# Short-sequence attention: larger load packets for q, k and v, paid for with more selector matmuls, and a reordered end

## The chip, the cores and the metric

One core of a Trainium2 chip runs the whole kernel. The metric is the device time of one execution in microseconds, lower is better. Executions of this kernel scatter by two to three per cent (148.55 to 153.12 us in one set of runs), and a run is called slow when it is more than 1.5% above the fastest run of the same kernel; comparisons use fast runs.

## The reference, cut to what matters

```python
# q, k, v: float32 [32, 12, 128, 64]: 384 heads of 128 positions by 64
scores = (1 / sqrt(64)) * q @ k.transpose(0, 1, 3, 2)
attn   = softmax(scores)            # over the last axis
out    = attn @ v                   # float32
```

Each head needs q, k and v read once (37.75 MB in all) and its result written once (12.58 MB). Nothing is reused between heads, so the kernel is a stream.

## The kernel before

A unit is eight heads, and there are 48 units. The loads convert float32 to bf16 on the way and are issued by POOL. A partition takes R = 8 consecutive rows of q or k (2 KB read in one piece) or RV = 4 rows of v (1 KB). Having several rows in one partition makes longer pieces, but it puts the rows in an order that the matmuls can't use directly. For q and k the transposes put that right. For v, PE multiplies with columns of the identity ("pick"), which gathers one row from each of the 32 partitions of a head into one 32-row tile; four such matmuls bring all its rows. These are the parts that matter here:

```python
R, RV = 8, 4                     # rows per partition: q and k, v
PERIOD, LOOP0, TRIPS = 8, 2, 5   # PE's program: steps 2..41 are a loop of 8 steps,
                                 # the others are written out
NQ, NVB, NO = 12, 2, 3           # buffers for q (and k), for v groups, for outputs

def order_v(m):                  # PE: bring v of one unit into row order
    ...
    for i in range(nh):          # nh = 4 // n, n units in the load group
        h = w * nh + i
        for r in range(RV):      # 4 matmuls of 512 columns for n = 4
            x = nc.tensor.matmul(
                t[r * SV:(r + 1) * SV, i, :, :],
                lhsT=pick[:, h * SV:(h + 1) * SV],
                rhs=v_b[g % NVB][:, :n * 2, r * D:(r + 1) * D],
                start=True, stop=True)

def tensor_step(u):              # cut: PE's order in one step
    transposes(u + 3)            # 8 matmuls, q or k of a coming unit
    order_v(u + 4)               # 4 matmuls
    scores(u + 1)                # 8
    values(u)                    # 32

# POOL, for a v load: its buffer must have been read by PE
if x >= NVB:
    last = sum(vgroups[:x - NVB + 1]) - 1
    g_.wait_ge(pe_act, ev_pe_act["V", last])
```

In a step, ACT copies the ordered v out of PSUM (`keep_v`) and takes the exponentials, and DVE copies the transposed q and k, pairs up the next ones and normalises. SP stores two units at a time. A v load needs a buffer that PE has finished ordering, and there are two such buffers of four units each. That is the link from PE back to the transfers.

The softmax here doesn't subtract the row's maximum and nothing guards it: scores larger than these inputs give would overflow.

## Time and profile before

| | before |
|---|---|
| time, median of three runs | 150.04 us (149.95 to 150.37) |
| span of the profiled execution | 147.9 us |
| PE instructions by the page (matmuls / weight loads) | 2528 / 2528 |
| DMA engines' time lost until 135 us, by fitted packet costs | 5.9 us, all of it before 50 us |

"Time lost" is worked out from the packet records: for each stretch of 5 us, 5 us less (packets in it x fitted cost) / 16 engines. The prediction explains the fit. A loss of zero means that the sixteen engines always had a packet to move. What bounds the kernel is in the page's slices and in the waits, which the prediction shows.

### The profile page before, as it was taken

How to read it: one execution, taken by the hardware profiler on the slowest of the kernel's cores; microseconds unless marked ns; L12 is line 12 of the kernel's file. 1: busy time of each engine (PE TensorE's matmuls, PEld its weight loads, DVE VectorE, ACT ScalarE, POOL GpSimd, SP SyncE). 2: the span in 40 equal slices, each digit the busy share in tenths (PEclk: the TensorE clock that was granted, in tenths of full speed). 3: DMA queues.
4: the chain of work that ended last, by engine and by line, in shares of the span. 5: the costliest groups of instructions: out<-in, count | busy, mean ns of one | idle time of the engine just before them, and what ended most of it. 6: DMA issues, size and time to landing. Idle time of an engine off the chain costs nothing. (4 is left out here: it accounts for less than half of the span.)

```text
span 147.9 us, 5753 instructions
## 1 busy us (share of the span) xinstructions
PE 99.3 (67%) x2528; PEld 65.8 (44%) x2528; DVE 91.1 (62%) x202; ACT 74.9 (51%) x97; POOL 47.3 (32%) x67
## 2 busy tenths in 40 slices
PE   0247779975298859719949929829819949984530
PEld 0234436553255536415736616516515725653420
DVE  1242347877188966727868937837927858897240
ACT  3005645658047857714746736725824746766510
POOL 6912727054009091270063090090093010010000
PEclk9999999999659996985796895996985796899555
DMA  1999999999999999999999999999999999997442
GB/s 14 197 180 200 149 185 221 223 210 254 244 211 235 203 248 246 248 233 223 239 226 241 243 227 233 246 225 232 243 228 233 237 224 244 236 283 230 145 136 71
DMA packets 38282, 31.59 MB, mean 214 GB/s; under 512 B 1408, under 2 KB 38272, under 8 KB 38272
## 3 DMA queue, kind: packets, MB, share of 16 engines
q0 software_dynamic: 25568, 18.88, 83.3%
q1 hardware_dynamic: 12704, 12.58, 29.3%
q8 instruction: 6, 0.10, 0.2%
q14 instruction: 4, 0.03, 0.1%
HBM read 37.75 MB, written 12.58 MB: 340 GB/s over the span
## 5 line engine op out<-in xcount | busy, mean ns | idle before, releaser
L214 PE MATMUL qk_ps<-ident,pair 128*128 128x128 bf16 x384 | 38.3, 260 | 32.6 <-PEq L204 32.6
L311 ACT CAST v_e<-v_ps 128x512 bf16<-128x512 f32 x48 | 28.2, 588 | 62.3 <-PE v_ps L229 62.3
L318 ACT ACTIVATE attnT<-s_ps 128x1024 bf16<-128x1024 f32 x48 | 49.3, 1027 | 3.6 <-PE s_ps L250 3.6
L214 PEld LDWEIGHTS qk_ps<-ident,pair 128*128 128x128 bf16 x384 | 29.1, 117 | 37.4 <-issue 36.0
L192 POOL DMA_DIRECT2D v_b<-in_v_dram x14 | 12.3, 882 | 81.4 <-PE v_ps L229 48.0
L352 DVE COPY qkT<-qk_ps 128x1024 bf16<-128x1024 bf16 x48 | 33.0, 688 | 8.1 <-PE qk_ps L214 8.0
L369 DVE TENSOR_TENSOR o_sb<-o_ps,recip 128x512 f32<-128x512 f32 x48 | 33.2, 691 | 1.7
L260 PE MATMUL o_ps<-v_e,attnT 128*32 128x65 bf16 x1536 | 25.0, 214 | 8.6 <-issue 5.2
L229 PE MATMUL v_ps<-v_b,pick 128*32 128x512 bf16 (+2 forms) x224 | 23.9, 448 | 2.4 <-PEq L204 2.4
L260 PEld LDWEIGHTS o_ps<-v_e,attnT 128*32 128x32 bf16 x1536 | 18.1, 108 | 15.8 <-issue 12.8
L250 PE MATMUL s_ps<-qkT 64*128 64x128 bf16 x384 | 22.9, 251 | 0.0
L366 DVE RECIPROCAL recip<-o_ps 128x8 f32<-128x8 f32 x48 | 9.8, 204 | 20.8 <-PE o_ps L260 19.9
L345 DVE COPY pair<-k_b 128x1024 bf16<-128x1024 bf16 x24 | 10.8, 451 | 17.4 <-DMA v_b<-in_v_dram 17.3
L250 PEld LDWEIGHTS s_ps<-qkT 64*128 64x128 bf16 x384 | 13.0, 106 | 13.7 <-issue 13.2
L178 POOL DMA_DIRECT2D k_b<-in_k_dram x24 | 18.0, 750 | 0.0
L174 POOL DMA_DIRECT2D q_b<-in_q_dram x24 | 17.6, 733 | 1.0 <-SPq L82 1.0
L345 DVE COPY pair<-q_b 128x1024 bf16<-128x1024 bf16 x24 | 10.1, 419 | 1.7 <-DMA q_b<-in_q_dram 1.7
L229 PEld LDWEIGHTS v_ps<-v_b,pick 128*32 128x32 bf16 x224 | 5.8, 102 | 10.1 <-issue 7.3
L311 ACT ACT_TABLE_LOAD x1 | 1.3, 1283 | 0.9 <-SPq L82 0.9
L383 DVE COPY pick<-ident 128x128 bf16<-128x128 bf16 x1 | 0.2, 227 | 2.0 <-POOL ident L167 2.0
L378 DVE MEMSET ident<- 128x64 uint32 x1 | 0.1, 112 | 1.0 <-SPq L82 1.0
L167 POOL TENSOR_SCALAR_AFFINE_SELECT ident<-ident 128x128 bf16<-128x128 bf16 x1 | 0.3, 312 | 0.1
(5 smaller groups left out, 0.7 us busy)
## 6 DMA issues: line engine op xcount, KB each, us to landing
out_dram<-o_sb SPq DMA_DIRECT2D x22, 512.0 KB, 7.8
q_b<-in_q_dram POOLq DMA_DIRECT2D x24, 256.0 KB, 14.0
k_b<-in_k_dram POOLq DMA_DIRECT2D x24, 256.0 KB, 15.2
v_b<-in_v_dram POOLq DMA_DIRECT2D x11, 512.0 KB, 12.2
out_dram<-o_sb SPq DMA_DIRECT2D x4, 256.0 KB, 4.6
v_b<-in_v_dram POOLq DMA_DIRECT2D x1, 256.0 KB, 5.8
v_b<-in_v_dram POOLq DMA_DIRECT2D x2, 128.0 KB, 9.7
```

The lines of the kernel that those rows point to most:

```text
L174: g_.dma_start(out=q_b[x % NQ][:], in_=qs[:, 2 * x:2 * x + 2, :]).then_inc(s_q[x % NQ], 16)
L178: g_.dma_start(out=k_b[x % NQ][:], in_=ks[:, 2 * x:2 * x + 2, :]).then_inc(s_k[x % NQ], 16)
L192: g_.dma_start(out=t, in_=src).then_inc(s_v[x % NVB], 16)
L214: i = nc.tensor.transpose(qk_ps[:, :, r4, jj, :], x[:, r].rearrange("p a d -> p (a d)"), ident[:])
L229: x = nc.tensor.matmul(t[r * SV:(r + 1) * SV, i, :, :], lhsT=pick[:, h * SV:(h + 1) * SV], rhs=v_b[g % NVB][:, :n * 2, r * D:(r + 1) * D], ...
L250: i = nc.tensor.matmul(s_ps[u % 2][:, a, h, :], lhsT=x[p, 1, 4 * w + h, :], rhs=x[p, 0, 4 * w + h, :], start=True, stop=True)
L260: i = nc.tensor.matmul(o_ps[h * SV:(h + 1) * SV, a, r * (D + 1):(r + 1) * (D + 1)], lhsT=x[:, a, h, r * SV:(r + 1) * SV], rhs=v_of(u, a, h ...
L311: nc.scalar.copy(v_e[m % NVE][:, :, :D], v_ps[:].rearrange("p (n e) -> p n e", e=D),).then_inc(act_pe, 1)
L318: nc.scalar.activation(out=attnT[u % NA][:].rearrange("p a h (r s j) -> p (a h r) s j", s=SP, j=J), in_=s_ps[u % 2][:].rearrange("p a h (r ...
L345: nc.vector.tensor_copy(pair[t % NP][:], src[s % NQ][:].rearrange("p a (r d) -> p r a d", d=D),).then_inc(dve_pe, 1)
L352: nc.vector.tensor_copy(qkT[s % NT][:, j].rearrange("p h x -> p (h x)"), qk_ps[:].rearrange("p h r j s -> p (h r j s)"),).then_inc(*((dve_ ...
L369: nc.vector.tensor_mul(o[:, :, w, :].rearrange("p a (r d) -> p a r d", d=D), o4[:, :, :, :D], r[:].unsqueeze(3).to_broadcast([128, 2, RV, D]),
```

## The change

Its intent is fewer and larger load packets. q and k go by 16 rows per partition for the forty units in the middle (4 KB pieces in place of 2 KB) and stay at 8 rows for the first and last four units; v goes by 8 rows (2 KB in place of 1 KB). With 8 rows in a partition only 16 partitions hold a head of v, and a 32-row tile has to be put together from two halves. So each ordering takes two accumulated matmuls per tile, each over half as many columns: 16 matmuls where there were 4. The last four units are reordered so that v comes last there. PE's loop starts at step 7 in place of step 2. Most stores of two units go out as two transfers in place of one, and the two-unit v groups have buffers of their own.

The core of the diff (most of the rest moves the same waits into an explicit list of operations; cuts are marked "..."):

```diff
-    R = 8
-    RV = 4
+    RO, SO = 4, S // 4
+    RV, SV = 8, S // 8
+    for R in [8] * 2 + [16] * ((NU - 8) // 4) + [8] * 2:
...
-    vgroups = [2] + [4] * ((NU - 4) // 4) + [1, 1]
+    vgroups = [2, 2] + [4] * ((NU - 8) // 4) + [2, 2]
-    PERIOD, LOOP0, TRIPS = 8, 2, 5
+    PERIOD, LOOP0, TRIPS = 8, 7, 4
-    NQ, NVB, NVE, NP, NT, NA, NO = 12, 2, 8, 4, 4, 4, 3
+    NQ, NVB, NVE, NP, NT, NA, NO = 6, 2, 8, 4, 4, 4, 3
...
+        nh = 8 // n
         for i in range(nh):
-            for r in range(RV):
-                x = nc.tensor.matmul(
-                    t[r * SV:(r + 1) * SV, i, :, :],
-                    lhsT=pick[:, h * SV:(h + 1) * SV],
-                    rhs=v_b[g % NVB][:, :n * 2, r * D:(r + 1) * D],
-                    start=True, stop=True)
+            for jv in range(2):
+                for r4 in range(4):
+                    x = nc.tensor.matmul(
+                        t[r4 * 32:(r4 + 1) * 32, i, :, :],
+                        lhsT=pick[:, w * nh + i, jv, :],
+                        rhs=v_b[v_slot(g)][:, :n, (4 * jv + r4) * D:(4 * jv + r4 + 1) * D],
+                        start=jv == 0, stop=jv == 1)
...
+    u = TAIL                     # the last four units, written out in a new order
+    ...
```

## The prediction

> **What bounds the kernel now.** I read the page's slices first, then its queue table, then the trace's packet records by size, then windows, waits and the timeline of the end. One unit is eight heads; there are 48.
>
> ```profile
> PE   0247779975298859719949929829819949984530
> DVE  1242347877188966727868937837927858897240
> PEclk9999999999659996985796895996985796899555
> DMA  1999999999999999999999999999999999997442
> ...
> q0 software_dynamic: 25568, 18.88, 83.3%
> q1 hardware_dynamic: 12704, 12.58, 29.3%
> ```
>
> The DMA row is full from the second slice to the thirty-sixth, while PE, DVE and ACT dip to 2 and 1 again and again. The two queues' packet times add to more than 100%, so packets of the loads (q0) and of the stores (q1) overlap, and a packet's own duration is not what it costs. To get the cost I counted packets by size (v: 512 B written from 1 KB read; q and k: 1 KB from 2 KB; stores: 1 KB) in 28 windows of 2.5 us between 60 and 130 us, and fitted 16 engines x 2.5 us = sum of count x cost. The fit gives 42.1 ns for a v packet, 79.9 for a q or k packet, 53.1 for a store packet, and misses a window by 0.008 us rms: the engines were never short of work there. Over the whole run this is 12,288 x (42.1 + 79.9 + 53.1) / 16 = 134.4 us of a 147.9 us span. Summed from the start, the time the engines lost is 5.9 us by 50 us (3.5 in the first five, before loads flow; 1.4 between 15 and 25), then nothing until 135 us.
>
> ```profile
> 60.00:130.00 70.00, 50.66 (x1329) 33.83 (x1314) 48.04 (x103) 38.63 (x52) 21.61 (x29) 0.80 1.24 235
> ```
>
> Columns: PE, PEld, DVE, ACT, POOL busy, then clock, DMA share and GB/s. In these 70 us no compute engine passes 73%; 52 matmuls a unit make 1329/52 = 25.6 units, 2.74 us each by this count (some records can be missing); the packet costs give 256 x 175.1 / 16 = 2.80 us a unit.
>
> ```profile
> POOL v_b L192 <- PE v_ps L229: 48.0, 8, 9.4
> ...
> PE qk_ps L214 <- PEq L204: 32.6, 30, 5.9
> ...
> DVE pair L345 <- DMA v_b<-in_v_dram: 17.3, 8, 3.4
> ```
> ```profile
> 120.91 0.43 DVE L345 COPY pair<-k_b 128x1024 bf16<-128x1024 bf16 x1 [1.69 <-DMA v_b<-in_v_dram]
> ...
> 124.24 0.62 PE L229 MATMUL v_ps<-v_b,pick 128*32 128x512 bf16 x4
> ...
> 124.79 0.61 PE L250 MATMUL s_ps<-qkT 64*128 64x128 bf16 x8
> ...
> 126.78 0.40 PE L229 MATMUL v_ps<-v_b,pick 128*32 128x512 bf16 x4
> ...
> 127.11 0.40 PE L250 MATMUL s_ps<-qkT 64*128 64x128 bf16 x8
> ...
> 133.58 0.61 PE L214 MATMUL qk_ps<-ident,pair 128*128 128x128 bf16 x8 [0.52 <-PEq L204]
> ...
> 143.20 0.69 DVE L369 TENSOR_TENSOR o_sb<-o_ps,recip 128x512 f32<-128x512 f32 x1
> ```
>
> The waits (us in total, times, longest) show the rhythm: POOL issues a v load only when PE has freed its buffer, DVE stalls some 2 us for v once per four units, and PE behind it. The timeline of the end (start us, us) shows the last of these. At 120.91 the copy that also waits for the last group of four v units starts: the last wait for a load. From there on compute sets the pace: 23.0 us to the last normalisation's end at 143.9, and 4.0 us more for its store and the program's end. So the end is (arrival of the last four-unit v group) + (compute that remains). PE shows two speeds: v ordering to scores takes 0.55 us at 124.24 and 0.33 us at 126.78. A full step is 2.6 us slow and 1.82 to 1.9 us fast, where DVE's 0.20 + 0.69 + 0.69 + 0.42 us per unit is the limit.
>
> **What the Trainium skill says.** "DMA: Bandwidth & Descriptors", section "Why small descriptors are slow (HBM only)": a fixed overhead of about 3 cycles per packet inside the engine. "Advanced Engine Details and Errata", section "DMA Bandwidth Details": 27.2 GB/s per engine, so 37.6 ns per KB read. The fit agrees: 42.1 and 79.9 split into 4.2 ns a packet and 37.8 ns per KB. "DMA: Bandwidth & Descriptors", section "Queues, rings and completion order": an engine goes round its queues packet by packet; no run here has shown yet what that does to larger packets. "TensorE: Matmul & The Clock Gate", section "Part 1: The HAM clock gate (the "warmup" mystery)": the array runs at half clock after an idle window of some 3.4 us; the granted clock of 0.80 and the two speeds above agree.
>
> **The change part by part.**
>
> 1. Load packets. Of 48 units, 40 take q and k by 16 rows (4 KB read) and 8 stay at 8 rows; v goes by 8 rows (2 KB). A 4 KB packet costs, by the split, 4.2 + 4 x 37.8 = 155.5 ns. Loads before: 12,288 x (42.1 + 79.9) / 16 = 93.7 us. After: v 6,144 x 79.9 = 491 us, q and k 5,120 x 155.5 = 796 us and 2,048 x 79.9 = 164 us, together 1,451 / 16 = 90.7 us. Gain 3.0 us. Bytes are unchanged, so halving the packets buys only the 4.2 ns each: this is the part where a hope from "half the packets" fails. Stores keep 1 KB packets: 12,288 x 53.1 / 16 = 40.8 us, unchanged.
>
> 2. Start. Before, the third v load waits for PE (issued at 13.7 us) and the engines lose 1.4 us around it. The new order has 16 units of q and k and 12 of v before the first load that waits. I take 1.9 us less lost.
>
> 3. Arrival of the last four-unit v group. Before (units 42 to 45), 46 units of v and 42 of q and k precede or are it: (11,776 x 42.1 + 10,752 x 79.9) / 16 = 84.7 us; with 34.3 units of stores counted by then (29.2) and 5.9 lost this is 119.8, and about 1.1 us of landing gives the 120.9 seen. After (units 40 to 43): 44 units of each, 83.0 us; one unit of stores fewer, 28.3; lost 4.0. Sum 115.3, with landing 116.4: 4.5 us earlier.
>
> 4. PE's v ordering. Four matmuls of 512 columns on four 32-column tiles become 16 of 256 (two accumulated per key block): twice the columns, so the 0.33 us fast becomes about 0.33 + 512/2.4 GHz = 0.55 us, and 0.55 slow becomes about 0.98. In the middle this is 44 x 0.2 to 0.4 us of PE time that lies under the DMA: a fast step becomes 1.95 us, a slow one 3.04, and four of them mixed about 9.9 us against 4 x 2.74 = 11.0 us of DMA (estimates from the rows above).
>
> 5. Compute after that arrival. One more step remains than before (37 to 43, then the tail). Steps 37 and 38: 1.95 each if fast, about 1 us more for each slow one. Steps 39 and 40 have no transposes: PE 0.55 + 0.33 + 0.45, ACT 0.59 + 1.02; 1.7 each. Steps 41 to 43 have no v ordering: 1.82 each. Sum 12.8 to 13.9, plus 0.6 to the first transposes. Tail from the last transposes: nine DVE steps (five normalisations of 0.93, the qkT copy 0.69, three v copies of about 0.66 moved there from ACT) and PE between them; walking the chain copy, values, normalise gives 10.2 us fast and about 11.4 slow, against 10.3 (133.58 to 143.9) before, which held two v orderings and not four. Total 23.6 to 25.9 against 23.0.
>
> Sum: 143.9 - 4.5 + (0.6 to 2.9) = 140.0 to 142.3; plus 4.0 for the store and end gives a span of 144.0 to 146.3; plus the 2.2 us between span (147.9) and time (150.04): 146.2 to 148.5. I take 147.1.
>
> **The rivals.**
>
> A: the descriptors were the bound, and half of them are gone. If a packet cost its recorded duration (60 and 98 ns median) the split would be 22 ns a packet, 36 a KB, and the loads would fall by about 16 us: 136 to 140. Against it stands the fit: the durations overlap and over-count, and 37.8 ns per KB leaves little to gain.
>
> B: PE takes over. If slow steps of 3.04 us become the rule, PE passes DMA's 2.74 us a unit and the middle grows by up to 0.3 x 40 = 12 us: 152 to 158. For it: the clock is 0.80 already. Against it: shorter waits mean fewer slow stretches, and in slices 9, 10 and others PE ran above 90%.
>
> C: the gain is real but eaten at the end: slower v ordering and four of them in the tail cost as much as the 4.5 us. 149 to 151. For it: everything after 120.9 us is compute, which the change does not shorten.
>
> D: 4 KB load packets push the 1 KB stores aside in the turn of queues; o_sb's three buffers fill and DVE waits. Stores took 7.8 us to land, and three buffers of two units leave some 11 us: a wait of a microsecond here and there, hidden while loads bound. Smaller than 1 us.
>
> **Range and chances.** Mechanism 1 is firm to 0.5 us, 2 and 3 to 1.5 us, 5 to 1.5 us. Together about 2.4 us either way, which covers C and part of B; A I give one in fifteen. Range 144.0 to 150.2. The 2% line lies at 147.04, just under my value, so chances: faster 0.49, same 0.46, slower 0.05.
>
> **What would show it.** Step 1: load packets near 157 ns of cost per 4 KB in a fit of windows, the loads' total near 91 us, DMA row still full. Step 2: no dip in GB/s near 15 to 25 us. Step 3: the last wait for v at about 116 us. Step 4: 16 matmuls per v ordering, and PE's busy time up by 10 to 20 us, waits for v smaller but still there. Step 5: from the last transposes to the end of the last normalisation 10 to 11.5 us. I would be wrong if the DMA row opened in the middle (B), if 4 KB packets cost much more or less than 155 ns, or if the DVE copy into 16-element runs took longer than 0.69 us.

## The result, and the profile after

| | before | after |
|---|---|---|
| time, median | 150.16 us (149.95 to 150.37) | 161.97 us (158.49 to 162.44) |
| ratio of fast runs | | 1.0615, 95% interval 1.0508 to 1.0722 |
| profiled span | 147.9 us | 156.3 us |
| DMA engines' time lost by 85 us | 5.9 us | 12.9 us |

A ratio here is the mean time of one kernel's fast runs over that of the other kernel's fast runs of the same rounds, so it isn't quite the ratio of the medians. After has two fast runs, 158.49 and 160.3 us; its other three took 161.7 to 162.4 at a granted clock that was no lower (0.89 to 0.91 against 0.88). Before ran at 0.81 to 0.86 in the sets below, so a lower clock is not what made after slow. The profile is of the fastest. The kernel became slower by some 6%, where 2% faster was predicted.

The page of the kernel after, the rows that answer to those of before (slices of 3.9 us, then the queues):

```profile
PE   0257776548198784879879497577598687587750
DVE  3345444448156693647988458557755985684570
PEclk9999999999758999677999969999969999955576
DMA  1999999999994999997999999999999999953043
GB/s 19 182 196 209 206 213 226 224 247 132 211 227 145 142 217 272 233 220 213 147 203 239 246 237 250 244 236 238 244 237 242 244 240 245 291 182 134 4 152 121
...
q0 software_dynamic: 13984, 18.88, 70.1%
q1 hardware_dynamic: 13024, 12.59, 27.0%
q8 instruction: 13, 0.21, 0.5%
```

The load queue's packets fell from 25568 to 13984, as intended. But the DMA row, full before until the thirty-sixth slice, opens in the middle, and the GB/s row falls to 132 and 142 to 147 where no slice from the sixth to the thirty-seventh went under 185. From about 80 us on it is full again. The last row is the queue that fetches instructions; before it had 6 packets by the page, now 13.

Two windows of each kernel give the size. The columns are the window, its length, busy time (and count) of PE, PEld, DVE, ACT and POOL, the granted clock, the DMA share and GB/s. Before:

```profile
80.00:130.00 50.00, 37.28 (x981) 24.80 (x978) 34.96 (x75) 28.40 (x38) 14.05 (x19) 0.81 1.23 235
25.00:80.00 55.00, 40.49 (x1064) 26.93 (x1052) 38.38 (x83) 31.16 (x41) 19.10 (x25) 0.83 1.23 232
```

After:

```profile
80.00:130.00 50.00, 37.79 (x1224) 26.60 (x1216) 34.08 (x75) 28.52 (x38) 11.60 (x16) 0.93 1.14 241
...
25.00:80.00 55.00, 39.44 (x1160) 27.38 (x1164) 33.00 (x73) 28.04 (x37) 8.72 (x12) 0.88 1.02 204
```

Between 80 and 130 us, with the engines saturated in both, the larger packets give 241 GB/s against 235, 2.6% more. That is the gain the prediction worked out (134.4 to 131.4 us, 2.2%). Between 25 and 80 us the rate is 204 against 232. At 52 and 64 matmuls a unit the PE counts make 1064/52 = 20.5 units before and 1160/64 = 18.1 after. PE issued 9% more matmuls in these 55 us and still got 2.3 units less done.

Why did the engines run dry? These are waits of the kernel after (engine, line, what it waited for: us in total, times, longest):

```profile
POOL v_b L425 <- PE v_ps L186: 86.6, 8, 21.0
...
DVE recip L267 <- DMA out_dram<-o_sb: 12.3, 8, 2.3
...
PE o_ps L223 <- issue: 11.5, 6, 3.3
...
DVE pair L249 <- DMA v_b<-in_v_dram: 0.4, 1, 0.4
```

DVE's wait for v, 17.3 us before, is all but gone: in the middle compute no longer waits for loads. It is the reverse. POOL waits up to 21 us for PE to free a v buffer, and it issues in order, so the q and k loads behind that v load wait too. In total POOL waited little longer than before (86.6 against 81.4 us); the difference is that before still had enough loads under way during its waits (9.4 us at most), and after had not. Two POOL stretches in the timeline of after (start, length, what it is, idle before it):

```profile
33.04 0.76 POOL L425 DMA_DIRECT2D v_b<-in_v_dram  x1 [21.00 <-PE v_ps L186]
33.79 0.72 POOL L440 DMA_DIRECT2D q_b<-in_q_dram  x1
34.48 0.74 POOL L440 DMA_DIRECT2D k_b<-in_k_dram  x1
48.66 0.76 POOL L425 DMA_DIRECT2D v_b<-in_v_dram  x1 [13.43 <-PE v_ps L186]
```

After the k load issued at 34.5 us no load was issued until 48.7 us, and the losses fall into the stretches 35 to 40, 45 to 50, 50 to 55, and again 70 to 75 and 75 to 80 us.

So PE was late. The timeline of PE in after, the groups of one step being transposes (L172), v ordering (L186), scores (L211) and values (L223):

```profile
32.10 0.62 PE L186 MATMUL v_ps<-v_b,sel 128*32 128x256 bf16 x16
32.66 0.40 PE L211 MATMUL s_ps<-qkT 64*128 64x128 bf16 x8
32.98 0.33 PE L223 MATMUL o_ps<-v_e,attnT 128*32 128x65 bf16 x19
35.52 0.29 PE L223 MATMUL o_ps<-v_e,attnT 128*32 128x65 bf16 x13 [2.21 <-issue]
...
36.30 0.62 PE L186 MATMUL v_ps<-v_b,sel 128*32 128x256 bf16 x16
...
39.30 0.31 PE L223 MATMUL o_ps<-v_e,attnT 128*32 128x65 bf16 x15
42.90 0.46 PE L223 MATMUL o_ps<-v_e,attnT 128*32 128x65 bf16 x17 [3.30 <-issue]
```
```profile
44.25 1.04 PE L186 MATMUL v_ps<-v_b,sel 128*32 128x256 bf16 x16
```

A values group is 32 matmuls that need the same inputs. Here it breaks off after 19 and after 15 of them, with no semaphore in between, and goes on 2.2 and 3.3 us later; "issue" says that the profile shows nothing that PE waited for. Each of these two stops has a 16 KB packet on the instruction queue in it: packets start at 33.24 and 40.68 us, where PE's last matmuls end at 33.32 and 39.60, take 0.95 us, and PE resumes 1.3 us after they end. From one stop to the next, PE's records (matmuls, weight loads and its sequencer's waits) number 256 each time, for all seven stops between 29 and 67 us: one stop per 16 KB block, at 64 bytes each. After the longer stop PE runs at about half speed for nearly two steps (v ordering takes 1.04 us at 44.25), after the shorter it doesn't (0.62 us at 36.30). The record of the granted clock goes to half at 41.36 us and back at 48.19, in stretches that are multiples of 3.41 us: the length agrees with the window of the clock gate that the prediction names, but the half clock came 1.8 us after PE had stopped, not after 3.4 us of idling.

The Trainium skill, "Runtime: NRT & Kernel Launch", section "Instruction fetch mechanics", says that instructions come in 16 KiB blocks of 256, fetched by a DMA queue of the sequencer's own, and that the cost is mostly hidden. The trace agrees on the block's size, and disagrees on the hiding: between 20 and 80 us there are seven such stops in after, 12.8 us together (idle time of PE that the timeline puts down to "issue", stops over 0.4 us).

Before had them too, but fewer:

```profile
39.62 0.35 PE L260 MATMUL o_ps<-v_e,attnT 128*32 128x65 bf16 x11 [3.73 <-issue]
```

That and one of 0.62 us are all between 20 and 80 us, because its loop begins at step 2 and, once inside it, PE runs code that is there already (no instruction packet between 45 and 133 us). After has 64 matmuls a step in place of 52 and enters the loop five steps later, so it fetches more.

The times at which units are normalised, from the trace, show where the loss builds up:

| unit | before, us | after, us | difference |
|---|---|---|---|
| 0 | 18.0 | 20.1 | +2.1 |
| 4 | 29.6 | 35.9 | +6.3 |
| 16 | 60.5 | 73.2 | +12.7 |
| 37 | 121.3 | 127.3 | +6.0 |
| 47 | 143.0 | 151.5 | +8.5 |

By unit 16 after is 12.7 us late. Before is paced by its transfers there and later, so after catches up in part until unit 37; what remains corresponds to the engine time that was lost for good. 7.0 us more lost, less the 2.3 us that larger packets save by then (3.0 x 37/48), is 4.7 of those 6.0 us. I have not placed the other 1.3. The last ten units add 2.5 us; the third set shows that they are a second place where the loss arises.

### The profile page after: what moved, and what is told of

Its sections match the earlier page's. It is cut to its first block, busy times and chain, and to the rows that moved or that the text cites. A ratio compares the mean times of both kernels' runs of the same rounds, so it can differ in the third digit from the quotient of the medians.

```text
span 156.3 us, 7154 instructions
## 1 busy us (share of the span) xinstructions
PE 106.6 (68%) x3200; PEld 76.4 (49%) x3200; DVE 93.2 (60%) x210; ACT 73.0 (47%) x94; POOL 31.0 (20%) x47
## 3 DMA queue, kind: packets, MB, share of 16 engines
q0 software_dynamic: 13984, 18.88, 70.1%
## 5 line engine op out<-in xcount | busy, mean ns | idle before, releaser
L232 ACT CAST v_e<-v_ps 128x512 bf16<-128x512 f32 x45 | 26.4, 588 | 68.4 <-PE v_ps L186 68.2
L172 PE MATMUL qk_ps<-ident,pair 128*128 128x128 bf16 x384 | 35.5, 247 | 18.6 <-PEq L524 18.2
L223 PE MATMUL o_ps<-v_e,attnT 128*32 128x65 bf16 x1504 | 23.8, 207 | 22.1 <-issue 11.5
L172 PEld LDWEIGHTS qk_ps<-ident,pair 128*128 128x128 bf16 x384 | 26.7, 110 | 23.3 <-issue 21.9
L186 PE MATMUL v_ps<-v_b,sel 128*32 128x256 bf16 (+1 forms) x864 | 34.4, 297 | 1.7 <-PEq L524 1.6
L267 DVE RECIPROCAL recip<-o_ps 128x8 f32<-128x8 f32 x47 | 9.6, 205 | 42.1 <-PE o_ps L223 26.5
L270 DVE TENSOR_TENSOR o_sb<-o_ps,recip 128x512 f32<-128x512 f32 x47 | 32.5, 692 | 1.6
L223 PEld LDWEIGHTS o_ps<-v_e,attnT 128*32 128x32 bf16 x1504 | 17.2, 103 | 30.7 <-issue 28.0
L425 POOL DMA_DIRECT2D v_b<-in_v_dram x14 | 10.7, 768 | 86.6 <-PE v_ps L186 86.6
L186 PEld LDWEIGHTS v_ps<-v_b,sel 128*32 128x32 bf16 x864 | 19.4, 109 | 8.1 <-issue 4.0
L211 PE MATMUL s_ps<-qkT 64*128 64x128 bf16 x384 | 21.8, 238 | 1.8 <-issue 1.3
L211 PEld LDWEIGHTS s_ps<-qkT 64*128 64x128 bf16 x384 | 12.2, 102 | 11.9 <-issue 11.6
L440 POOL DMA_DIRECT2D q_b<-in_q_dram x14 | 10.2, 726 | 1.0 <-SPq L93 1.0
L440 POOL DMA_DIRECT2D k_b<-in_k_dram x14 | 10.3, 740 | 0.0
L232 DVE CAST v_e<-v_ps 128x512 bf16<-128x512 f32 x2 | 1.4, 693 | 2.1 <-PE v_ps L186 1.9
## 6 DMA issues: line engine op xcount, KB each, us to landing
v_b<-in_v_dram POOLq DMA_DIRECT2D x10, 512.0 KB, 10.2
```

The lines of the kernel that those rows point to most:

```text
L172: i = nc.tensor.transpose(p[:, :, r4, jj, :], x[:, r].rearrange("p a d -> p (a d)"), ident[:])
L186: x = nc.tensor.matmul(t[r4 * 32:(r4 + 1) * 32, i, :, :], lhsT=pick[:, w * nh + i, jv, :], rhs=v_b[v_slot(g)][:, :n, (4 * jv + r4) * D:(4 ...
L211: i = nc.tensor.matmul(t[:, a, h, :], lhsT=x[p, 1, 4 * w + h, :], rhs=x[p, 0, 4 * w + h, :], start=True, stop=True)
L223: y = nc.tensor.matmul(t[h * SO:(h + 1) * SO, a, r * (D + 1):(r + 1) * (D + 1)], lhsT=x[:, a, h, r * SO:(r + 1) * SO], rhs=v_e[m % NVE][:, ...
L232: return put(v_e[m % NVE][:, :, :D], v_bank(m).rearrange("p (n e) -> p n e", e=D))
L267: nc.vector.reciprocal(r[:], o4[:, :, :, D]).then_inc(s_r, 1)
```

## The experiments

Theory 1: the load packets behave as predicted, but PE became late in its first sixteen units, because the changed v ordering makes its program larger, and lateness starves the loads. Rivals: the stores (three output buffers), the columns of the added matmuls, the reordered end, the 16-row loads of q and k, the 8-row loads of v themselves. Sixteen kernels were run, in four sets, each beside runs of the kernel before on the same chip. Six of the profiles are of slow executions (marked "slow" in the table at the end, or said in the text), so stops and unit times from them are read with care.

**First set.** The kernel before with its loop starting later, so that more of PE's code is written out:

```diff
-    PERIOD, LOOP0, TRIPS = 8, 2, 5
+    PERIOD, LOOP0, TRIPS = 8, 10, 4
```

> The kernel before with its PE loop entered at step 10 with 4 trips instead of at step 2 with 5: the same work in the same order, eight more steps of PE code written out, all in front of the loop. Theory 1 (PE instruction fetch: in the changed kernel PE stops about 2.4 us in the middle of a group of matmuls once per 16 KB of code that it runs for the first time): about 8 x 110 x 64 B = 56 KB more code, so 10 or 11 instruction packets of 16 KB where the kernel before has 7, three or four more stops before 65 us, the DMA engines idle in the first half, and a time 4 to 10 us longer (154 to 160 us). Theory 2 (the loss comes from what the change does to matmuls or to packets): no change, 150 us.

Measured: 149.31 us, ratio 0.998 (0.986 to 1.010), result right. In the profile, which is of a slow execution, the stops came (11.8 us of them between 20 and 80 us, ten instruction packets as expected), unit 16 fell 6 us behind, and the engines lost only 1.6 us more. Theory 1 in this form missed: here a late PE was absorbed, since the transfers set the pace.

The kernel after with its loop starting earlier (`LOOP0` 3 in place of 7):

> The changed kernel with its PE loop entered at step 3 instead of 7, still 4 trips: the same work and the same amount of code, but four steps of it moved from in front of the loop to behind it. Theory 1: two fewer stops before 65 us, unit 16 normalised some 4 to 6 us earlier than the 73 us of the changed kernel; the code moved behind the loop costs less there because the DMA engines bound that stretch; the time falls by 2 to 5 us (154 to 158 us). Theory 2: no change, 158 to 162 us.

Measured: 164.11 us, ratio 1.100, and the result was wrong (relative error 0.33). The loop repeats fixed addresses, and the 8-row units at the start need others. The longer written-out end had stops of 3.8 and 2.0 us where no transfer hides them. As a test of fewer stops it is void.

Five output buffers in place of three:

```diff
-    NQ, NVB, NVE, NP, NT, NA, NO = 6, 2, 8, 4, 4, 4, 3
+    NQ, NVB, NVE, NP, NT, NA, NO = 6, 2, 8, 4, 4, 4, 5
```

> The changed kernel with five output buffers instead of three. If the normalisations' waits for stores (12.3 us in 8 waits, all after 80 us) are what costs time, they vanish and the time falls by 5 us or more. If the DMA engines bound that stretch anyway (they lost nothing between 80 and 130 us by the packet costs), the waits move to the v loads and the time falls by less than 2 us.

Measured: 160.83 us, ratio 1.077 (1.061 to 1.092). The waits for stores (12.3 us in after) are gone, 10.3 us of waits for v came in their place, and the time did not improve. The stores only took over a wait that the saturated engines impose anyway.

The second matmul of each pair over a quarter of its columns (wrong):

```diff
+                    c = D if jv == 0 else D // 4
-                        t[r4 * 32:(r4 + 1) * 32, i, :, :],
+                        t[r4 * 32:(r4 + 1) * 32, i, :, :c],
...
-                        rhs=v_b[v_slot(g)][:, :n, (4 * jv + r4) * D:(4 * jv + r4 + 1) * D],
+                        rhs=v_b[v_slot(g)][:, :n, (4 * jv + r4) * D:(4 * jv + r4) * D + c],
```

> The changed kernel with the second matmul of each accumulated pair cut to a quarter of its columns (wrong result on purpose): the number of PE instructions is unchanged, the columns streamed for v fall from 1024 to 640 a unit and column tile. If PE's longer v ordering is the cause of the loss, the time falls by 4 us or more. If instruction fetch is, the stops stay at about 2.4 us each and the time falls by at most 2 us.

Measured: 160.28 us, ratio 1.0725 (1.059 to 1.086). So it is not the columns that cost. The timeline shows how short the ordering became:

```profile
37.27 0.46 PE L187 MATMUL v_ps<-v_b,sel 128*32 128x256 bf16 x16
37.66 0.40 PE L212 MATMUL s_ps<-qkT 64*128 64x128 bf16 x8
```

From v ordering to scores it took 0.39 us, against 0.55 in after and 0.33 in before (at full clock). Over 48 units that is at most 2.9 us more than before, and the loss is still whole. Its granted clock was lower than after's (0.82 against 0.88), which could hide part of what the columns cost.

**Second set.** The kernel after with the loop eight steps later (`LOOP0, TRIPS = 15, 3`):

> The changed kernel with eight more steps of PE code written out in front of the loop (loop from step 15, 3 trips, instead of step 7, 4 trips). If compute that runs late through instruction fetch is what lets the DMA engines run dry here, four more stops of 2 to 3 us follow between 65 and 95 us, the engines idle longer and the time grows by 4 to 9 us (164 to 170 us). If a late PE is absorbed by the transfers, as it was when the kernel before got the same eight steps, the time stays within 2 us of 160.5.

Measured: 163.77 us, ratio 1.090 (1.079 to 1.101). More written-out code costs about 2.7% here (the time is just under the range expected), in the direction of theory 1; the same edit cost the kernel before nothing.

The v loads from the fifth on placed eight steps later in POOL's order, with two more q and k buffers, so that a v load that waits for PE doesn't hold back q and k:

```diff
-        loads.append((vstep_of[m] + 0.5 if m in vstep_of else NU + m, "v", g))
+        loads.append((vstep_of[m] + (0.5 if g < 4 else 8.5) if m in vstep_of else NU + m, "v", g))
```

> The changed kernel with the fifth and later v loads queued eight steps later among the loads, and eight q and k buffers instead of six: up to eight more units of q and k are fetched before the loads wait for PE to free a v buffer. PE's code and all compute are unchanged. If the idle time of the DMA engines between 30 and 80 us (8 us of it, by the packet costs) is part of what costs the time, it falls by half or more and the time falls by 3 to 7 us (154 to 158 us). If compute alone sets the time, nothing changes (160 us).

Measured: 155.58 us, ratio 1.034 (1.021 to 1.047). Its window between 25 and 80 us:

```profile
25.00:80.00 55.00, 40.55 (x1118) 27.88 (x1118) 31.20 (x69) 26.01 (x35) 8.73 (x12) 0.80 1.13 229
```

The rate is 229 GB/s against 204, the time lost by 85 us is 5.9 as in before, and nearly half of the loss is gone. But unit 16 is as late as ever (75.7 us), and compute, now the limit, ends 3.5 us later than before's. So the starving is a consequence of the late PE, and the way in which about half of the loss comes about.

The regular end in place of the reordered one:

> The changed kernel with the regular order of steps to the end: v of the last four units ordered three steps ahead like the others, on ACT, in the usual banks. The changed kernel takes 24.2 us from the normalisation of unit 37 to that of unit 47, the kernel before 21.7. If the reordered tail with four v orderings in it costs that, the time falls by 2 to 4 us. If the tail's length comes from waits for stores and cold PE, it stays or grows by up to 2 us.

Measured: 159.88 us, ratio 1.0635 (1.053 to 1.074). The reordered end is neutral, so later kernels use the regular one, which is simpler.

q and k by 8 rows throughout, with 12 buffers:

```diff
-    for R in [8] * 2 + [16] * ((NU - 8) // 4) + [8] * 2:
+    for R in [8] * (NU // 2):
```

> The changed kernel with q and k by 8 rows per partition throughout (12 buffers of half the size), v by 8 rows and the reordered tail as they are. By the packet costs the loads need 1.4 us more of the engines. If the 16-row loads and their two-part transposes at the start delay the first units (unit 4 is normalised at 35.9 us against 29.6 before), the time falls by 3 us or more. If v by 8 rows with its 16 matmuls causes the loss, it stays within 2 us of 160.5.

Measured: 158.98 us, ratio 1.048 (1.034 to 1.062). In the profile (a slow execution) units 0 to 4 come early again, and unit 16 is still at 72.2 us. The median lies within 2 us of 160.5 and the ratio's interval overlaps after's, so q and k are not shown to be the main cause.

**Third set, the v part alone.** v put back to 4 rows and 4 matmuls (ordered four steps ahead, as in before), q and k by 16 rows, regular end:

```diff
-    RV, SV = 8, S // 8
+    RV, SV = 4, S // 4
...
-            for jv in range(2):          # 16 matmuls
...
+            for r4 in range(4):          # 4 matmuls
...
```

> The change with v put back to 4 rows per partition and 4 selector matmuls per ordering, and the regular end; q and k keep 16 rows. Theory 1 (the extra matmuls and code of v by 8 rows make the first sixteen units late, so the loads starve): most of the loss is gone, 149 to 153 us, and engine time lost before 80 us falls from 12.9 to 5 to 8 us. Rival (the longer 16-row q and k loads delay the first units and that lead is what is missing): stays at 157 to 161 us.

Measured: 153.03 us, ratio 1.010 (0.999 to 1.021), against 1.0635 with v by 8 rows and the same end. The v part is some five sixths of the loss. The expected drop in lost engine time, to 5 to 8 us, did not come: it is 9.9 us in the profile (a slow execution).

This pair also shows where the loss arises. At unit 16 the version with 16 matmuls is 4.2 us later than the one with 4 (74.5 against 70.3 us), at unit 37 only 1.1 us, and at unit 47 6.9 us: its last ten units take 23.6 us against 17.8. Most of those steps lie behind PE's loop and are written out again; with 16 matmuls PE makes two stops in them (0.9 and 1.9 us), with 4 none over 0.4 us, and with 16 its clock is at half from 144.5 us on (in the other from 145.7, when its work is nearly done). So besides the first 80 us the end is a place where the added matmuls cost time.

The kernel before, its v ordering padded with 12 tiny matmuls of 16 columns, which the real ones overwrite (the result is right), and the loop starting later as in the first run:

```diff
+        for i in range(12 // nh):
+            nc.tensor.matmul(
+                v_ps[:SV, i * 16:(i + 1) * 16], lhsT=pick[:, :SV],
+                rhs=v_b[g % NVB][:, 0, :16], start=True, stop=True)
```

> The kernel before, its v ordering padded with 12 tiny matmuls (result right) and its loop starting later, so that PE's program has the changed kernel's instruction count per step and written-out size; all loads as before. Theory 1 (code size and the stops for fetching it are enough): 154 to 160 us, mid-group stops of 10 us or more, engine time lost before 80 us above 10 us. Rival (the loads' sizes and the lead they set matter too): 149 to 152 us with the same stops.

Measured: 156.47 us, ratio 1.035 (1.026 to 1.045). The padding alone, the loop where it was:

> The kernel before with the padded v ordering alone, loop starting where it did. Theory 1: 150 to 153 us, because the loop starts at its second step and most code is fetched once early. Rival (the 12 extra matmuls themselves cost, whatever the code): 154 to 160 us, and the padded orderings lengthen every step in the profile.

Measured: 153.94 us, ratio 1.017 (1.007 to 1.027), between the two ranges expected. The padding does lengthen each step: from v ordering to scores now takes 0.62 us at full clock, more than after's 0.55, since the tiny matmuls come on top of the real ones. So it adds time to each ordering as well as instructions. The page row and the window of the padded kernel with the later loop:

```profile
DMA  2999999999999996999499999999999999998451
...
q8 instruction: 12, 0.20, 0.5%
```
```profile
25.00:80.00 55.00, 40.30 (x1098) 28.07 (x1091) 31.99 (x70) 26.22 (x36) 16.26 (x22) 0.81 1.10 201
```

Every load of this kernel is as in before, and yet the DMA row opens in the middle and the rate falls to 201 GB/s. The added matmuls and code alone bring about the picture of after. Later loop alone 0.998, padding alone 1.017, both 1.035: it looks as if the slack absorbs either of them better than both, though with intervals of about 0.01 either way this is not sure.

v back and the loads ahead, together:

> v back to 4 rows and 4 matmuls, regular end, q and k by 16 rows, and the v loads queued 8 steps later in their engine's order so that q and k are fetched ahead. Theory 1: 147 to 151 us, no loss of engine time between 50 and 80 us. Rival (16-row q and k themselves cost): 154 to 158 us like the version with v by 8 rows and the same queueing.

Measured: 154.6 us, ratio 1.026 (1.017 to 1.036). The time lies in the rival's range (154 to 158), against theory 1. The engines were kept busy (5.3 us lost by 85, 1.3 of it after 50), but compute was later than without the new queueing (unit 16 at 75.1 us against 70.3). Whether that comes of putting v later, as I think, or of 16-row q and k, was not tested apart. In this version loads ahead of a late PE did not help.

**Fourth set, loads or instructions.** The padding of 12 matmuls on the version with v by 4 rows:

> v by 4 rows and its 4 matmuls as in the version that gave 1.01 of before, plus 12 tiny 16-column matmuls per v ordering (result right). If the number of PE instructions is the whole cost of v by 8 rows: ratio 1.05 to 1.07 and 13 us or more of mid-group stops. If the loads of v by 8 rows also cost: 1.02 to 1.035, as the padding did in the kernel before.

Measured: 158.93 us, ratio 1.050 (1.039 to 1.060), against 1.010 without the padding: 12 tiny matmuls a unit bring 4.0 of the 5.4 points that v by 8 rows costs, with the loads unchanged. Stops were 9.0 us between 20 and 80 us (in a slow execution), not the 13 that I had said, so their sum does not explain the time by itself.

The counterpart: v loaded by 8 rows, but ordered by 4 matmuls of 512 columns. This is wrong, since the sums leave out half of the rows.

```diff
-        nh = 8 // n
...
+        nh = 4 // n
...
-            for jv in range(2):
-                for r4 in range(4):
...
+            for r4 in range(4):
+                x = nc.tensor.matmul(
+                    t[r4 * 32:(r4 + 1) * 32, i, :, :],
+                    lhsT=pick[:, w * nh + i, 0, :],
+                    rhs=v_b[v_slot(g)][:, :n, r4 * 2 * D:(r4 + 1) * 2 * D],
...
```

> v loaded by 8 rows but ordered by 4 matmuls of 512 columns per key group (wrong on purpose, the sums leave out half of the rows), regular end. If the number of PE instructions is the cost of v by 8 rows: ratio 1.00 to 1.02. If the loads of v by 8 rows cost: 1.04 to 1.06.

Measured: 150.22 us (147.66 to 151.22), and before 150.35 in the same rounds: the whole loss is gone with the larger loads in place. The medians give 0.999, but three of the four runs count as slow; the one fast run gives 0.985 against before's five (147.66 against 149.89 us). Its page and window, of a slow execution:

```profile
DMA  1999999999999999999999999999999999942371
...
q0 software_dynamic: 13984, 18.88, 72.6%
```
```profile
25.00:80.00 55.00, 41.55 (x1092) 27.26 (x1084) 38.47 (x82) 32.17 (x43) 10.95 (x15) 0.84 1.12 232
80.00:130.00 50.00, 36.85 (x984) 24.54 (x984) 34.42 (x74) 29.16 (x39) 9.42 (x13) 0.83 1.15 246
```

The same 13984 load packets as after, and 232 GB/s in the early window where after had 204. The gain from larger packets is there (246 GB/s later), while the first units come 2 to 3 us later (unit 4 at 32.5 us against 29.6). Whether the gain reaches the end (0.985 or 0.999) one fast run does not settle.

q and k by 8 rows again, now with all four buffers for transposed pairs in use; the earlier version had used two of them, which made it an unfair test:

```diff
-        return s % 2 + (2 if supers[s][0] == 8 else 0)
+        return s % 4
```

> q and k by 8 rows throughout with all four transposed-pair buffers in use (the earlier version with 8 rows used only two of the four), v by 8 rows. If the two buffers held that version back: ratio 1.02 to 1.035. If v by 8 rows is what costs: 1.04 to 1.05 as before.

Measured: 159.96 us, ratio 1.068 (1.057 to 1.079). The two buffers held nothing back. With v by 8 rows, q and k by 8 or by 16 rows makes no clear difference (1.048 and 1.068 against 1.0635).

v by 4 rows, q and k by 8 rows for the first eight units, the loop from step 15, meant as a version that could beat both:

> v by 4 rows with 4 matmuls, q and k by 8 rows for the first eight units and 16 after, regular end, loop from step 15: the candidate that could beat both. The first normalisation should come at 18 to 19 us instead of 22. If the late start was the cost of q and k by 16 rows: ratio 0.985 to 1.00. If not: 1.01.

Measured: 153.46 us, ratio 1.024 (1.016 to 1.031). The first normalisation is back at 18.1 us, but with more code written out it has 13.0 us of stops between 20 and 80 us (in a slow execution), and it is no better. No correct version beat the kernel before.

From the profiled execution of each kernel, the main ones in a row:

| kernel | matmuls | stops, 20 to 80 us | unit 16 at | lost by 85 us | ratio |
|---|---|---|---|---|---|
| before | 2528 | 4.4 us | 60.5 us | 5.9 us | 1 |
| v by 8 rows, 4 matmuls (wrong; slow) | 2528 | 5.1 | 64.4 | 6.3 | (0.999) |
| before, later loop (slow) | 2528 | 11.8 | 66.6 | 7.5 | 0.998 |
| before, padded | 3074 | 6.4 | 65.5 | 9.2 | 1.017 |
| v by 4 rows, q and k by 16 (slow) | 2528 | 10.3 | 70.3 | 9.9 | 1.010 |
| before, padded, later loop | 3074 | 13.2 | 73.0 | 13.8 | 1.035 |
| v by 4 rows, padded (slow) | 3104 | 9.0 | 74.7 | 13.8 | 1.050 |
| after | 3200 | 12.8 | 73.2 | 12.9 | 1.0615 |

"slow" marks a profile of a slow execution; the ratios are of fast runs except the one in brackets. Counts are as recorded, and a few records are missing. Within each set of loads, lateness at unit 16 and lost engine time go up when matmuls are added. The stops alone do not order the table, and the loads are not without effect: with the same matmuls, the two kernels with 16-row q and k are 1.2 and 1.5 points slower than their counterparts with the loads of before and the later loop, each within the noise or at its edge.

## Why the prediction was wrong

Predicted were 147.1 us (144.0 to 150.2), with a chance of 0.05 for slower; the fast runs were 158.5 and 160.3 us.

1. Load packets: right. The fitted 155.5 ns for a 4 KB packet leaves at most 0.1 us of each 5 us unexplained between 85 and 130 us (0.01 us in seven of the nine stretches), and 241 against 235 GB/s is the gain that was worked out. A fit with free costs on the version with v by 8 rows and 4 matmuls (85 to 124 us) gives 155.5 again. Rival A was rightly set aside.

2. Start: half right. The dip near 15 to 25 us is gone and the loss by 30 us is 4.4 against 5.4 us. But the first units came 2 us later, which the step did not look at.

3. Arrival of the last group of v: wrong. "Lost 4.0" was 12.9 us. The last four-unit load was issued at 113.95 us, since PE freed its buffer late, and landed at 124.2, not at the 116.4 us of the sum. Nor was it the last wait any more: compute was later still.

4. PE's v ordering: this is the step that failed, and not in its size. From v ordering to scores takes 0.55 us at full clock and 0.98 at half, exactly as forecast (its 512 columns at 2.4 GHz agree with the trace, where transposes of 128 columns start 55 to 56 ns apart). What failed is that this "lies under the DMA". In the first 80 us PE was late, and the DMA engines waited for the buffers that it frees. The step left out what 12 more matmuls and weight loads a unit add to PE's program, which has to be fetched where it is not in the loop: seven stops of 12.8 us in place of two of 4.4. With fewer columns nothing changed (1.0725); with fewer matmuls the loss went away; with added matmuls of 16 columns most of it came without any change of loads. PE's busy time, up by 7.3 us (99.3 to 106.6, where 10 to 20 were forecast), does not show it.

5. The end: 12.3 us from the last transposes at 140.1 us to the end of the last normalisation at 152.4, against 10.2 to 11.4 predicted. The granted clock was 0.61 between 140 and 156 us and three instruction packets fall into the stretch. Too low by 0.9 us, and minor.

Of the rivals, B came nearest: PE did take over, and the time lies just above its 152 to 158. Its reason was not the one that was weighed (slow steps throughout), and the argument against it ("shorter waits mean fewer slow stretches") looked at the average of the middle, where the transfers indeed still bound. Most of the loss arises in the first 80 us, and part in the last ten units. The prediction's own support there was misread: its page shows 7 and 5 for PE in slices 9 and 10, and the nines are in slices 7, 8, 12 and others. Rival C missed in number (149 to 151), and the reordered end was neutral (1.0635 without it). Rival D showed up in the waits (12.3 us for stores) and cost nothing.

Shown is that the added matmuls of the v ordering, and not v's larger loads, the stores or the reordered end, make up most of the loss, and that the idle transfers are about half of how it acts. That it is their number, and not the time that each ordering takes, rests on one pair: 16 matmuls with fewer columns (0.39 us an ordering, the loss whole) against 4 matmuls (0.33 us, no loss), both with v by 8 rows and both wrong (their ends differ, which was neutral). The padding can't tell the two apart, since its orderings took 0.62 us. Not settled is how the cost divides between the stops for fetching, the half clock that follows a long stop, and the rest: padding gave 1.7% with few stops and 3.5% with the later loop's many, while the later loop alone cost nothing. Nor is the 1% that q and k by 16 rows cost by themselves (interval 0.999 to 1.021) sure to be anything.

## What to carry to other kernels

Count what a layout change adds in instructions and not only in columns or bytes: here the v part cost some 8 us (1.0635 against 1.010), and its larger packets were worth only 1.6 of the 3.0 us gained in the transfers (an estimate from the fitted costs: 12,288 packets of 42.1 ns against 6,144 of 79.9). A kernel that is bound by transfers in its middle can still be bound by PE at the start and at the end, where its code runs for the first time, and lateness at the start turns into idle transfers as soon as loads wait for buffers that PE frees. When engine rows have slack, ask in which stretch.

## What the Trainium skill lacked or had wrong

- "Runtime: NRT & Kernel Launch", section "Instruction fetch mechanics", calls the crossing of a 16 KiB block mostly hidden. Here the fetch packets of 16 KB took 0.88 to 1.4 us, and PE stopped for up to 3.3 us around them in the middle of a group of matmuls: seven stops and 12.8 us between 20 and 80 us in after, two and 4.4 us in before (one of 3.7 us). Some fetches showed no stop.
- No page that I read says that the recorded duration of a DMA packet overstates what it costs while the engines are full: 4 KB load packets were recorded at 172 ns (median) and cost 155.5 ns in the saturated windows; before, 60 and 98 ns were recorded where 42.1 and 79.9 fitted.
